# A shorter norm for the differential heads, and a part of the output projection moved ahead of the transposes

## The chip, the cores and the metric

The kernel runs on one core of one Trainium2 chip. Its time is the device time of that core in microseconds, as the median of three runs. One further execution was recorded by the hardware profiler; its rows give the times of single instructions, counted from the start of the recorded span.

## What is computed

One layer of an encoder over 528 rows (16 learned tokens, then 512 of the input) and 1,024 channels: two kinds of attention side by side, each with eight heads, then gates, an output projection and a feed-forward block. The change lies in the second kind, the differential attention: two softmax maps per head, one taken from the other, and a norm over the 128 channels of each head's result.

```python
def diff_attn_block(q, k, v, lam, slopes, qpos, kpos, qcid, kcid):
    s = einsum('bhcqd,bhckd->bhcqk', q, k) * (DF_HEAD_DIM ** -0.5)
    s = where(mask, s + bias, -inf)
    p = softmax(s, axis=-1)
    w = p[:, :, 0] - lam * p[:, :, 1]
    return einsum('bhqk,bhkd->bhqd', w, v)
...
o_df = rmsnorm(o_df, subln_g[l]) * (1.0 - lam_init)      # over the 128 channels of a head
y_sb = o_sb @ w_br_sb[l]
y_df = o_df @ w_br_df[l]
gates = sigmoid(xn @ w_gate[l] + b_gate[l])
merged = gates[:, :, 0] * y_sb + gates[:, :, 1] * y_df
h = h + merged @ w_out[l]
```

## The kernel before

**Matrix products.** Every product is made of high and low parts: `mm3` issues three matmuls (L296 high by high, L297 low by high, L298 high by low). Weights come from DRAM by SP's queue into one of three buffers `wst`; ACT casts the high part `wh` (L78, 128x1024), and DVE subtracts it from the weights to get the low part `wl` (L81). Both go to four buffers each.

**The order.** After a start whose order is written out, the instructions are handed to a scheduler, which orders each engine's by priority (mostly the order of the code) and by the times that it reckons. The code interleaves two streams. A head (`df_head`, a generator) makes its scores, maps and weighted sums, and stops at several places to yield a number. The loop over the heads then emits so many *units* of other work: the halves of the query, key and value projections of the head after it, and the parts of one projection unit `y`, which multiplies earlier heads' outputs by a block of `w_br_df` (`y_units`, four output blocks of six matmuls, 128x512; ACT copies each block out, L816, and POOL's queue sends it to DRAM, L818 or L820). `turn` turns the value projection. After each unit that a yield asks for stands a `tick`; every second one issues a background transfer on POOL's queue (L151, weights for the feed-forward part, mostly 512 KB), which waits for the last of ACT's casts when it was issued.

**A differential head.** `scores(0)` to `scores(2)` and `scores3` make the scores of four blocks of queries (L726 and L727 on PE), add the bias and take the maximum (L730 on DVE). `maps` takes the exponentials (L754 on ACT) and combines the two maps with DVE (L757 to L760, the last of them the combination `pr`, 528 columns wide for the last block). `turned` transposes the combined probabilities on PE (nine L581, then L582); the rest of its outputs are `a_h` (L591, ACT), `a_l` (L592, DVE) and the small corner `a_s` (`stk` L587, L598 on DVE, L601 on POOL). `av` makes the weighted sums (L604 to L614). Then the norm: `of` is the copy of the sums out of PSUM (L782), `sq` its square, split into `sqh` and `sql`, and two matmuls with the constant `ones_r` (L789, L790) add the squares over the 128 partitions. That second piece waits in the list `late` until the next head's first yield. Line L719 prepares the next head's bias on POOL, and L709 copies each of the two key components to the other 64 partitions by POOL's queue (264 KB each), once DVE's last L706 of that component is done; the next head's scores need them.

**The loop** (L1049 to L1066 of the file): in head 7, the last, there is no next head, so its units are its `y` unit and halves of the gates' products.

```python
        yield 3 if h < NH - 1 else 2
        turned()
        yield 2
        ps = av()
...
                units = units + more[0:1] + [turn] + more[1:]
...
            for n in head(h, d, o[0][:, h % 2], o[1][:, h % 2]):
                for _ in range(min(n, len(units))):
                    units.pop(0)()
                    tick(*RATE[br])
            for u in units:
                u()
```

The units of a head are four halves (query, key), two of the value projection's, and then, around `turn`, the two halves of `y`: each half is two output blocks. The yields ask for 1, 1, 1, 3 and 2 of these nine, and the last follows the head. The heads are counted from 0, so that head 4 is the fifth.

Of the kernel before, what the change touches and what calls it, by code (L numbers as in the profile page):

```python
# [9 lines left out]
F32 = mybir.dt.float32  # L10
F32R = mybir.dt.float32r
# [5 lines left out]
P = 128  # L17
D = 1024
SEQ = 512
# [22 lines left out]
def block_kernel(ctx: ExitStack, tc: tile.TileContext, x, meta, norm_mix_g, w_in, w_gate, b_gate,  # L42
# [34 lines left out]
    def split(hi, lo, src, lo_eng=None, hi_copy=None, after=None):  # L77
        cast["last"] = (hi_copy or nc.scalar.copy)(hi, src)  # L78
        if after:
            behind(cast["last"], after)  # L80
        cast["lo"] = (lo_eng or nc.vector).tensor_tensor(lo, src, hi.bitcast(F32), op=ALU.subtract)  # L81
# [634 lines left out]
    def df_head(h, d, o_h, o_l):  # L716
        q, k = d["q"], d["k"]
        bias = ap_.tile([P, L], F32, tag="bias", name="bias")
        nc.gpsimd.tensor_scalar(bias, dist, -(2.0 ** -(h + 1)), None, op0=ALU.mult)  # L719
        mx = small.tile([P, NQ, 2], F32, tag="mx", name="mx", bufs=2)  # L720
        ls = small.tile([P, NQ, 2], F32, tag="ls", name="ls", bufs=2)
        prs = [ap_.tile([P, 2, 144 + t * P], F32, tag=f"w{t}", name="pr") for t in range(NQ)]

        def score(o, t, c, k0, k1):
            qs = slice(t * P, (t + 1) * P)
            nc.tensor.matmul(o, lhsT=q[c][:, qs], rhs=k[c][:, 0, k0:k1], start=True, stop=False)  # L726
            nc.tensor.matmul(o, lhsT=q[c][:, qs], rhs=k[c][:, 1, k0:k1], start=False, stop=True)  # L727

        def biased(t, c, zz, po, bb):
            nc.vector.tensor_tensor_reduce(po, zz, bb, scale=1.0, scalar=-3.0e38, op0=ALU.add, op1=ALU.max,  # L730
                                           accum_out=mx[:, t, c:c + 1])

        def scores(t):
            n = 144 + t * P
            z = z_tile()
            for c in range(2):
                score(z[:, c, 0:max(n, 256)], t, c, 0, max(n, 256))
            for c in range(2):
                biased(t, c, z[:, c, 0:n], prs[t][:, c], bias[:, L - n:L])
            maps(t)  # L740

        def scores3(c):
            two = lambda v: v.rearrange("p (a b) -> p a b", a=2)
            z = z_tile()
            for hf in range(2):
                score(z[:, hf, 0:HL], 3, c, hf * HL, (hf + 1) * HL)
            biased(3, c, z[:, :, 0:HL], two(prs[3][:, c]), two(bias))

        def maps(t):
            pr = prs[t]  # L750
            nm = small.tile([P, 2], F32, tag="nm", name="nm")
            nc.vector.tensor_scalar(nm, mx[:, t], -1.0, None, op0=ALU.mult)
            for c in range(2):
                nc.scalar.activation(pr[:, c], pr[:, c], AF.Exp, bias=nm[:, c:c + 1], accum_out=ls[:, t, c:c + 1])  # L754
            with tc.high_priority(offset=EVAC):
                rc = small.tile([P, 2], F32, tag="rc", name="rc")
                nc.vector.reciprocal(rc, ls[:, t])  # L757
                nc.vector.tensor_tensor(rc, rc, cn, op=ALU.mult)
                nc.vector.tensor_scalar(pr[:, 0], pr[:, 0], rc[:, 0:1], None, op0=ALU.mult)
                nc.vector.scalar_tensor_tensor(pr[:, 0], pr[:, 1], rc[:, 1:2], pr[:, 0], op0=ALU.mult, op1=ALU.add)  # L760

        scores(0)
        scores(1)
        yield 1
        if late:
            late.pop(0)()
        scores(2)
        yield 1
        scores3(0)
        yield 1  # L770
        scores3(1)
        maps(3)
        turned, av = attn_out(lambda t, k0, k1: prs[t][:, 0, k0:k1], d, 64)
        yield 3 if h < NH - 1 else 2
        turned()
        yield 2
        ps = av()
        of = ap_.tile([P, SEQ], F32, tag="of", name="of")
        sq = ap_.tile([P, SEQ], F32, tag="sq", name="sq")
        sqh = ap_.tile([P, SEQ], F32R, tag="a_h", name="sqh")  # L780
        sql = ap_.tile([P, SEQ], F32R, tag="a_l", name="sql")
        nc.scalar.copy(of, ps)  # L782
        eng = nc.gpsimd if h < NH - 1 else nc.vector
        eng.tensor_tensor(sq, of, of, op=ALU.mult)
        split(sqh, sql, sq, lo_eng=eng)

        def norm():
            pv = tr_tile()
            nc.tensor.matmul(pv, lhsT=ones_r, rhs=sql, start=True, stop=False)  # L789
            nc.tensor.matmul(pv, lhsT=ones_r, rhs=sqh, start=False, stop=True)  # L790
            nc.scalar.activation(sq, pv, AF.Ln, bias=eps_c)
            cast["norm"] = nc.scalar.activation(sq, sq, AF.Exp, scale=-0.5)
            nc.vector.scalar_tensor_tensor(sq, pv, var_max, sq, op0=ALU.is_le, op1=ALU.mult)
            nc.vector.tensor_tensor(of, of, sq, op=ALU.mult)
            nc.scalar.activation(o_h, of, AF.Copy, scale=g_sub)
            nc.vector.scalar_tensor_tensor(o_l, of, g_sub, o_h.bitcast(F32), op0=ALU.mult, op1=ALU.subtract)

        late.append(norm)


    def y_units(name, i, o):

        def unit(fs):
            wh, wl = weights((name, i))
            for f in fs:
                ps = mm_tile()
                cs = slice(f % 4 * P, (f % 4 + 1) * P)
                mm3(ps, [(wh[:, k, cs], wl[:, k, cs], o[0][:, k], o[1][:, k]) for k in range(2)])
                if y_out:
                    ys = y_out[0][:, y_count[0] % KT]  # L810
                elif y_count[0] % 2:
                    ys = ap_.tile([P, SEQ], F32, tag="ys", bufs=2, name="ys")
                else:
                    ys = gate_tile(0)
                y_count[0] += 1
                nc.scalar.copy(ys, ps)  # L816
                if i < 2:
                    nc.gpsimd.dma_start(y_part[name][f], ys)  # L818
                else:
                    nc.gpsimd.dma_start(y_part[name][f], ys, accum_op=ALU.add)  # L820

        f0 = i % 2 * 4
        return [lambda: unit((f0, f0 + 1)), lambda: unit((f0 + 2, f0 + 3))]

    def gate(br, f, dst, func):
        def evac(ps):
# [200 lines left out]
    for br in range(2):  # L1027
        name, head = (("y_sb", sb_head), ("y_df", df_head))[br]
        if br:
            nc.gpsimd.memset(a_s, 0.0)  # L1030
            y_out.append(xtp.tile([P, KT, SEQ], F32, tag="y_sb", name="y_out"))
        for h in range(NH):
            if (br, h) == (0, 0):
                tB["t"] = opool.tile([P, 2, 2, 4, HL], F32R, tag="y_df", name="tB", bufs=1)
                sums = sum_units()
            if (br, h) == (0, 3):
                df_loads()
            if (br, h) == (0, 4):
                df_constants()
            if h % 2 == 0:  # L1040
                o = [opool.tile([P, 2, SEQ], F32R, tag=t, name=t) for t in ("o_h", "o_l")]
            if h + 1 < NH:
                nd, units, turn = (sb_units, df_units)[br](h + 1)
            elif br == 0:
                nd, units, turn = df_units(0)
            else:
                units, turn = [], None
            more = todo.pop(0) if todo else []
            if br == 0 and h < 2:  # L1049
                more = gate_out(h)  # L1050
            if turn is None:
                sg0 = [gate_tile(br) for br in range(2)]
                units = more + gate(0, 1, sg0[0], AF.Identity) + gate(1, 1, sg0[1], AF.Identity)
            else:
                units = units + more[0:1] + [turn] + more[1:]
            if (br, h) == (0, 0):
                for i, u in enumerate(sums):
                    units[i] = lambda a=units[i], b=u: (a(), b())
# [5 lines that stand above are left out]
                u()  # L1064
            d = nd
            if h % 2:  # L1066
                todo += [y_units(name, h - 1 + i, o) for i in range(2)]
    sg1 = [gate_tile(br) for br in range(2)]
    units = gate(0, 2, sg1[0], AF.Identity) + gate(1, 2, sg1[1], AF.Identity)
    units[0]()  # L1070
    late.pop(0)()
    for u in units[1:]:
        u()
    for units in todo:
        for u in units:
            u()
    for sg in sg0 + sg1:
        behind(nc.scalar.activation(sg, sg, AF.Sigmoid), "norm")
# [500 lines left out]
```

## Time and profile before

| | |
|---|---|
| runs | 932.18 us median of 3 (930.78 to 932.35) |
| the profiled execution | 930.21 us, of which the recorded span is 928.4 us |
| PE (matmul) | busy 916.8 us, 99% of the span, 6009 instructions |
| DVE | busy 741.2 us, 80% |
| ACT | busy 593.0 us, 64% |
| POOL | busy 171.6 us, 18% |
| granted TensorE clock | 0.999 |

The busy time of PE is modelled, since its matmuls are pipelined: two that follow each other without a gap are shown as overlapping, and the time that one costs is read from the distance between two starts. A row of the timeline gives the start, the length, the engine, the line, the operation with its output and inputs, and in brackets the idle time just before it and what ended it. The rows of the chain of waits have a start, a length, the engine, a tile, a line and a count. The rows by line and form give how often an instruction came, its shortest, median and longest time in nanoseconds, and from when to when.

### The profile page before, as it was taken

The page shows a single profiled execution, that of the slowest core. Times are in us where ns is not written, and L with a number is a line of the kernel's source. Part 1 is how long each engine was busy: PE and PEld are TensorE (multiplying, and loading weights), DVE is VectorE, ACT ScalarE, POOL GpSimd, SP SyncE. Part 2 cuts the span into 40 slices and gives each one's busy share as a digit, 9 for nine tenths or more (in the row PEclk, how much of TensorE's full clock was granted, in tenths as well). Part 3 has the DMA queues.
Part 4 walks back from the last instruction along what each step waited for, and adds up shares of the span by engine and source line. Part 5 has one row for each costly group of instructions (what it writes and reads, how often), then busy time and mean ns, then how long its engine had stood idle before and what let it go on. Part 6 is the DMA issues. An engine that isn't in the chain of part 4 may idle for free.

```text
span 928.4 us, 16121 instructions
## 1 busy us (share of the span) xinstructions
PE 916.8 (99%) x6009; PEld 834.1 (90%) x6010; DVE 741.2 (80%) x1453; ACT 593.0 (64%) x1136; POOL 171.6 (18%) x207
## 2 busy tenths in 40 slices
PE   8999999999999999999999999999999999999997
PEld 5999999998999899998988888899999999988886
DVE  7988877776687777977773787899888888799975
ACT  7665676676666766767665554776565655576554
POOL 4000121222333344344512000001100000000013
PEclk9999999999999999999999999999999999999999
DMA  8525698779776878799987774437744343276542
GB/s 253 143 74 159 147 211 202 168 168 257 185 203 157 218 180 195 172 206 179 207 207 173 214 271 155 123 87 182 172 122 128 91 133 96 91 272 195 192 148 91
DMA packets 155824, 158.42 MB, mean 171 GB/s; under 512 B 6465, under 2 KB 117218, under 8 KB 155746
## 3 DMA queue, kind: packets, MB, share of 16 engines
q1 hardware_dynamic: 132690, 101.61, 35.9%
q0 software_dynamic: 22896, 55.72, 28.9%
q8 instruction: 47, 0.77, 0.3%
q14 instruction: 31, 0.25, 0.1%
q10 hardware_dynamic: 160, 0.07, 0.0%
HBM read 133.64 MB, written 50.86 MB: 199 GB/s over the span
## 4 chain that ended last, share of the span: by engine, by line
PE 92%; DVE 4%; ACT 2%; issue 1%; DMA 0%; ACTq 0%; DVEq 0%
PE mm L296 22%; PE mm L297 22%; PE mm L298 22%; PE z L296 7%; PE z L297 7%; PE z L298 7%; PE z L581 2%; PE z L727 1%; PE z L726 1%; DVE wl L81 1%; PE tr L537 1%; DVE hres L1236 0%; ACT wh L78 0%; PE mm L889 0%; DMA wst<-in_w_ffn_up_dram 0%
## 5 line engine op out<-in xcount | busy, mean ns | idle before, releaser
L297 PE MATMUL mm<-xT_l,wh 128*128 128x264 f32 (+2 forms) x656 | 213.4, 325 | 0.5
L296 PE MATMUL mm<-xT_h,wh 128*128 128x264 f32 (+2 forms) x656 | 213.4, 325 | 0.5 <-ACT xT_h L932 0.5
L298 PE MATMUL mm<-xT_h,wl 128*128 128x264 f32 (+2 forms) x656 | 212.6, 324 | 0.0
L81 DVE TENSOR_TENSOR wl<-wst,wh 128x1024 fp32r<-128x1024 f32 (+1 forms) x147 | 163.2, 1115 | 27.7 <-ACT wh L78 27.3
L78 ACT CAST wh<-wst 128x1024 fp32r<-128x1024 f32 (+1 forms) x147 | 141.5, 966 | 58.8 <-PE mm L297 37.3
L297 PEld LDWEIGHTS mm<-xT_l,wh 128*128 128x128 f32 x656 | 123.4, 188 | 10.2 <-DVE xT_l L933 1.3
L298 PEld LDWEIGHTS mm<-xT_h,wl 128*128 128x128 f32 x656 | 123.5, 188 | 10.0
L296 PEld LDWEIGHTS mm<-xT_h,wh 128*128 128x128 f32 x656 | 123.4, 188 | 10.0 <-ACT xT_h L932 0.9
L296 PE MATMUL mm<-hT_h,wh 128*128 128x256 f32 x304 | 83.8, 277 | 0.3 <-ACT hT_h L1193 0.3
L298 PE MATMUL mm<-hT_h,wl 128*128 128x256 f32 x304 | 84.0, 277 | 0.0
L297 PE MATMUL mm<-hT_l,wh 128*128 128x256 f32 x304 | 83.9, 277 | 0.0
L296 PEld LDWEIGHTS mm<-hT_h,wh 128*128 128x128 f32 x304 | 56.9, 188 | 0.7 <-ACT hT_h L1193 0.5
L297 PEld LDWEIGHTS mm<-hT_l,wh 128*128 128x128 f32 x304 | 57.0, 188 | 0.0
L298 PEld LDWEIGHTS mm<-hT_h,wl 128*128 128x128 f32 x304 | 57.0, 188 | 0.0
L730 DVE CUSTOM_DVE_ANT_0 pr<-z,bias 128x144 f32<-128x144 f32 (+3 forms) x64 | 30.9, 502 | 30.5 <-PE z L727 28.5
L296 PE MATMUL mm<-o_h,wh 128*128 128x512 f32 x128 | 51.1, 399 | 0.0
L297 PE MATMUL z<-wl,da 128*128 128x512 f32 (+1 forms) x132 | 50.3, 381 | 0.2 <-DVE wl L81 0.2
L296 PE MATMUL z<-wh,da 128*128 128x512 f32 (+1 forms) x132 | 50.2, 380 | 0.0
L298 PE MATMUL z<-wh,da 128*128 128x512 f32 (+1 forms) x132 | 50.2, 380 | 0.0
L297 PE MATMUL mm<-o_l,wh 128*128 128x512 f32 x128 | 50.1, 391 | 0.0
L298 PE MATMUL mm<-o_h,wl 128*128 128x512 f32 x128 | 50.0, 391 | 0.0
L1481 POOL TENSOR_TENSOR outs<-hres,gF 128x512 f32<-128x512 f32 x4 | 6.2, 1549 | 217.2 <-DVE hres L1467 210.3
(388 smaller groups left out, 2509.9 us busy)
## 6 DMA issues: line engine op xcount, KB each, us to landing
wst<-in_w_in_dram SPq DMA_DIRECT2D x40, 512.0 KB, 6.0
ds<-in_w_ffn_down_dram POOLq DMA_DIRECT2D x30, 512.0 KB, 6.4
wst<-in_w_ffn_gate_dram SPq DMA_DIRECT2D x22, 512.0 KB, 3.9
wsu<-in_w_ffn_up_dram SPq DMA_DIRECT2D x20, 512.0 KB, 4.0
wst<-in_w_gate_dram SPq DMA_DIRECT2D x16, 512.0 KB, 5.0
y_df<-y_out POOLq DMA_DIRECT2D x32, 256.0 KB, 7.5
slots<-ds SPq DMA_DIRECT2D x13, 512.0 KB, 3.3
os<-in_w_out_dram POOLq DMA_DIRECT2D x12, 512.0 KB, 4.7
```

Of the source, the lines that this page charges most:

```text
L78: cast["last"] = (hi_copy or nc.scalar.copy)(hi, src)
L81: cast["lo"] = (lo_eng or nc.vector).tensor_tensor(lo, src, hi.bitcast(F32), op=ALU.subtract)
L296: nc.tensor.matmul(ps, lhsT=ah, rhs=bh, start=(start and i == 0), stop=False, skip_group_check=skip)
L297: nc.tensor.matmul(ps, lhsT=ah, rhs=bl, start=False, stop=False, skip_group_check=skip)
L298: nc.tensor.matmul(ps, lhsT=al, rhs=bh, start=False, stop=(stop and i == n - 1), skip_group_check=skip)
L537: nc.tensor.transpose(pt[:, j * P:(j + 1) * P], vT[:, j * P:(j + 1) * P], ident)
L581: nc.tensor.transpose(pt[:, (t - j) * P:(t - j + 1) * P], blocks(t, j * P, (j + 1) * P), ident)
L726: nc.tensor.matmul(o, lhsT=q[c][:, qs], rhs=k[c][:, 0, k0:k1], start=True, stop=False)
L727: nc.tensor.matmul(o, lhsT=q[c][:, qs], rhs=k[c][:, 1, k0:k1], start=False, stop=True)
L730: nc.vector.tensor_tensor_reduce(po, zz, bb, scale=1.0, scalar=-3.0e38, op0=ALU.add, op1=ALU.max, accum_out=mx[:, t, c:c + 1])
L1481: nc.gpsimd.tensor_tensor(outs[t][:, D1], hres[:, t, D1], gF[:, D1], op=ALU.mult)
```

## The change

Three things are done.

1. **The norm of heads 0 to 6.** Both halves of the partitions are squared apart: ACT squares `of[0:64]` into `sq2`, DVE squares `of[64:128]` into `sq[0:64]`, and DVE adds the two. ACT casts the high part of the 64 rows into `sqh[0:64]`, and DVE writes the low part into `sqh[64:128]`. One tile then holds both parts, and one matmul with `ones_r` adds them up. POOL has no part in it any more. Head 7 keeps square, split and two matmuls over all partitions.
2. **The projection unit.** In the differential branch it comes in three parts, of one, two and one output blocks. Every head now yields 4 ahead of `turned` (3 before, and 2 in head 7), so that the first block is emitted ahead of the transposes, the next two with `turn` between transposes and weighted sums, and the last after these. The list `todo` holds the arguments of a unit instead of the unit.
3. **The gates.** The first half of the gate product (0, 2) goes into the units of head 7.

With the larger yield a head has nine `tick`s instead of eight, and so two heads have nine background transfers instead of eight.

```diff
         turned, av = attn_out(lambda t, k0, k1: prs[t][:, 0, k0:k1], d, 64)
-        yield 3 if h < NH - 1 else 2
+        yield 4
         turned()
         yield 2
         ps = av()
...
-        sql = ap_.tile([P, SEQ], F32R, tag="a_l", name="sql")
         nc.scalar.copy(of, ps)
-        eng = nc.gpsimd if h < NH - 1 else nc.vector
-        eng.tensor_tensor(sq, of, of, op=ALU.mult)
-        split(sqh, sql, sq, lo_eng=eng)
+        halved = h < NH - 1
+        if halved:
+            A, B = slice(0, 64), slice(64, P)
+            sq2 = ap_.tile([P, SEQ], F32, tag="a_l", name="sq2")
+            nc.scalar.activation(sq2[A], of[A], AF.Square)
+            nc.vector.tensor_tensor(sq[A], of[B], of[B], op=ALU.mult)
+            nc.vector.tensor_tensor(sq[A], sq[A], sq2[A], op=ALU.add)
+            cast["last"] = nc.scalar.copy(sqh[A], sq[A])
+            cast["lo"] = nc.vector.tensor_tensor(sqh[B], sq[A], sqh[A].bitcast(F32), op=ALU.subtract)
+        else:
+            sql = ap_.tile([P, SEQ], F32R, tag="a_l", name="sql")
+            nc.vector.tensor_tensor(sq, of, of, op=ALU.mult)
+            split(sqh, sql, sq)
 
         def norm():
             pv = tr_tile()
-            nc.tensor.matmul(pv, lhsT=ones_r, rhs=sql, start=True, stop=False)
-            nc.tensor.matmul(pv, lhsT=ones_r, rhs=sqh, start=False, stop=True)
+            if not halved:
+                nc.tensor.matmul(pv, lhsT=ones_r, rhs=sql, start=True, stop=False)
+            nc.tensor.matmul(pv, lhsT=ones_r, rhs=sqh, start=halved, stop=True)
...
-    def y_units(name, i, o):
+    def y_units(name, i, o, parts=((0, 1), (2, 3))):
...
-        return [lambda: unit((f0, f0 + 1)), lambda: unit((f0 + 2, f0 + 3))]
+        return [lambda fs=fs: unit([f0 + f for f in fs]) for fs in parts]
...
-            more = todo.pop(0) if todo else []
+            more = y_units(*todo.pop(0), *(((0,), (1, 2), (3,)),)[0:br]) if todo else []
...
-                units = more + gate(0, 1, sg0[0], AF.Identity) + gate(1, 1, sg0[1], AF.Identity)
+                sg1 = [gate_tile(br) for br in range(2)]
+                third = gate(0, 2, sg1[0], AF.Identity)
+                units = more + gate(0, 1, sg0[0], AF.Identity) + gate(1, 1, sg0[1], AF.Identity) + third[0:1]
             else:
-                units = units + more[0:1] + [turn] + more[1:]
+                units = units + more[0:1 + br] + [turn] + more[1 + br:]
...
-    units = gate(0, 2, sg1[0], AF.Identity) + gate(1, 2, sg1[1], AF.Identity)
+    units = third[1:] + gate(1, 2, sg1[1], AF.Identity)
```

Behind the changed lines the numbers shift: the first line of the norm is L782 before and L781 after, the norm's last matmul L790 and L800, the copy of an output block L816 and L826.

At three places the order of the engines is shown. The first is PE's order at the transposes of head 4, before and then after; `o_h` and `o_l` are the outputs of earlier heads, so their rows are the projection unit's.

```order
L298 MATMUL mm<-xT_h,wl 128x264
L581 MATMUL z<-ident,pr 128x128 x9
L582 MATMUL z<-ident,pr 128x128
L296 MATMUL mm<-o_h,wh 128x512
L297 MATMUL mm<-o_l,wh 128x512
L298 MATMUL mm<-o_h,wl 128x512
```

```order
L298 MATMUL mm<-xT_h,wl 128x264
L296 MATMUL mm<-o_h,wh 128x512
L297 MATMUL mm<-o_l,wh 128x512
L298 MATMUL mm<-o_h,wl 128x512
L296 MATMUL mm<-o_h,wh 128x512
L297 MATMUL mm<-o_l,wh 128x512
L298 MATMUL mm<-o_h,wl 128x512
L581 MATMUL z<-ident,pr 128x128 x9
```

Six matmuls of the projection now stand between the last value projection and the first transpose.

The second is DVE's order in the same place, from the last but one weight subtraction before the probabilities to the row after their combination L760, before and then after.

```order
L81 TENSOR_TENSOR wl<-wst,wh 128x1024
L706 SCALAR_TENSOR_TENSOR dqk<-mm,dqk 64x264
L757 RECIPROCAL rc<-ls 128x2
L587 TENSOR_TENSOR stk<-pr,stk 64x16
L758 TENSOR_TENSOR rc<-rc,cn 128x2
L598 STREAM_TRANSPOSE a_s<-stk 32x32
L759 TENSOR_SCALAR pr<-pr,rc 128x528
L706 SCALAR_TENSOR_TENSOR dqk<-mm,dqk 64x264
L760 SCALAR_TENSOR_TENSOR pr<-pr,rc 128x528
```

```order
L81 TENSOR_TENSOR wl<-wst,wh 128x1024
L587 TENSOR_TENSOR stk<-pr,stk 64x16 x2
L598 STREAM_TRANSPOSE a_s<-stk 32x32 x4
L757 RECIPROCAL rc<-ls 128x2
L598 STREAM_TRANSPOSE a_s<-stk 32x32 x2
L758 TENSOR_TENSOR rc<-rc,cn 128x2
L706 SCALAR_TENSOR_TENSOR dqk<-mm,dqk 64x264
L759 TENSOR_SCALAR pr<-pr,rc 128x528
L81 TENSOR_TENSOR wl<-wst,wh 128x1024
L760 SCALAR_TENSOR_TENSOR pr<-pr,rc 128x528
L706 SCALAR_TENSOR_TENSOR dqk<-mm,dqk 64x264
```

More of the corner's rows and one more weight subtraction stand ahead of L760, and the last L706, which the second key copy follows, stands behind it.

The third is POOL's order from head 4's bias to its corner, before and then after; the rows L709 are the two key copies.

```order
L719 TENSOR_SCALAR bias<-dist 128x528
L151 DMA ds_2_97<-in_w_ffn_down_dram 256x1x512
L709 DMA dqk<-dqk 64x1056 x2
L601 CAST a_sr<-a_s 128x256
```

```order
L719 TENSOR_SCALAR bias<-dist 128x528
L709 DMA dqk<-dqk 64x1056
L151 DMA ds_8_100<-in_w_ffn_down_dram 256x1x512
L709 DMA dqk<-dqk 64x1056
L601 CAST a_sr<-a_s 128x256
```

A background transfer now stands between the two copies. Around the copy `of` of head 6, ACT's order changes in the same manner: before, the cast of the squares `sqh` came directly behind the copy, and now the square `sq2` and a cast of weights stand between them.

More of the change, by code (lines that the diff above doesn't have):

```diff
@@ L1066, in block_kernel @@
             if h % 2:
-                todo += [y_units(name, h - 1 + i, o) for i in range(2)]
-    sg1 = [gate_tile(br) for br in range(2)]
-    units = gate(0, 2, sg1[0], AF.Identity) + gate(1, 2, sg1[1], AF.Identity)
+                todo += [(name, h - 1 + i, o) for i in range(2)]
+    units = third[1:] + gate(1, 2, sg1[1], AF.Identity)
     units[0]()
@@ L1073, in block_kernel @@
         u()
-    for units in todo:
-        for u in units:
+    for args in todo:
+        for u in y_units(*args):
             u()
```

## The prediction

> **What bounds the kernel.** I read the page first, then PE's waits and the windows of the differential heads, then the timelines of one head (head 4, the fifth of eight) on PE, DVE, ACT and POOL.
>
> ```profile
> span 928.4 us, 16121 instructions
> PE 916.8 (99%) x6009; PEld 834.1 (90%) x6010; DVE 741.2 (80%) x1453; ACT 593.0 (64%) x1136; POOL 171.6 (18%) x207
> ...
> PE 92%; DVE 4%; ACT 2%; issue 1%; DMA 0%; ACTq 0%; DVEq 0%
> ...
> 361.50:391.00 29.50, 29.49 (x194) 27.00 (x193) 22.94 (x67) 20.65 (x49) 12.08 (x15) 1.00 0.84 187
> 450.00:476.00 26.00, 26.00 (x136) 22.21 (x136) 18.47 (x60) 19.11 (x47) 11.95 (x14) 1.00 1.08 223
> ```
>
> PE is busy 99% of the span and ends the chain for 92% of it. The window rows give busy time of PE, PEld, DVE, ACT, POOL, then granted clock (1.00), DMA share and GB/s: in head 4 PE never idles, DVE works 22.9 of 29.5 us, and in head 6 the DMA share is 1.08. So only two things move the end: fewer PE instructions, and holes in PE's stream. In a dense stream a matmul is worth the distance between starts, not its shown length:
>
> ```profile
> 463.10 0.39 PE L789 MATMUL tr<-sql,ones_r 128*128 128x512 f32 x1
> 463.33 0.39 PE L790 MATMUL tr<-sqh,ones_r 128*128 128x512 f32 x1
> 463.56 0.34 PE L726 MATMUL z<-dqk 128*128 128x400 f32 x1
> ```
>
> 0.39 us long each, but 0.23 apart. The holes are at the transposes L581. The chain has these runs, of which the one at 272.83 (head 0) did not wait:
>
> ```profile
> 272.83 0.98 PE z L581 x9
> 302.20 1.18 PE z L581 x9
> 331.87 1.10 PE z L581 x9
> 361.37 0.33 PE z L581 x3
> 361.70 0.87 PE z L581 x6
> 391.07 1.10 PE z L581 x9
> 420.57 1.17 PE z L581 x9
> 450.23 1.10 PE z L581 x9
> ...
> 476.21 0.49 PE L581 MATMUL z<-ident,pr 128*128 128x128 f32 x3
> 477.12 0.88 PE L581 MATMUL z<-ident,pr 128*128 128x128 f32 x6 [0.42 <-DVE pr L760]
> 477.83 0.27 PE L582 MATMUL z<-ident,pr 128*128 128x128 f32 x1
> ```
>
> Heads 1 to 6 lose 0.20, 0.12, 0.22, 0.12, 0.19 and 0.12, together 0.97 us, against 0.98. Head 7 takes 477.83 - 476.21 = 1.62 for the nine, 0.64 too long. What they wait for is DVE's last combination of the probabilities, L760.
>
> **The change, part by part.**
>
> *One norm matmul less in heads 0 to 6.* 7 x 0.23 = -1.6 us, straight off PE's stream. The Trainium skill ("TensorE: Matmul & The Clock Gate", section Back-to-back issue gap) gives a sustained 131 ns for 512 columns and 216 ns isolated, so the term would be -0.9 or -1.5 by it; the trace's 0.23 decides.
>
> *Three half-height DVE operations and an ACT square for two POOL operations.* Half height saves no time:
>
> ```profile
> L699 DVE SCALAR_TENSOR_TENSOR dqk<-mm,dqk 64x512 fp32r<-64x512 f32 x2 | 1.4, 688 | 0.1
> L784 DVE TENSOR_TENSOR sq<-of x1: 693/693/693, 483.6 to 483.6; 128x512 f32<-128x512 f32 x1
> L78 ACT CAST sqh<-sq x8: 620/620/622, 281.0 to 484.3; 128x512 fp32r<-128x512 f32 x8
> L1240 ACT ACTIVATE sq<-hres x8: 627/632/634, 579.8 to 599.9; 128x512 f32<-128x512 f32 x8
> 371.42 0.31 DVE L730 CUSTOM_DVE_ANT_0 pr<-z,bias 128x144 f32<-128x144 f32 x1 [4.06 <-PE z L727]
> 386.90 1.22 DVE L81 TENSOR_TENSOR wl<-wst,wh 128x1024 fp32r<-128x1024 f32 x1
> 390.47 0.77 DVE L760 SCALAR_TENSOR_TENSOR pr<-pr,rc 128x528 f32<-128x528 f32 x1
> 390.91 1.26 PE L581 MATMUL z<-ident,pr 128*128 128x128 f32 x9
> ```
>
> So 3 x 0.69 = 2.1 us more on DVE per head (25.0 of 29.5 us) and 0.63 on ACT; POOL's share is idle time won for nothing. Square and addition fall into DVE's 4.06 us of idleness before L730; the subtraction (0.69) does not, and delays the probabilities behind it.
>
> *The first quarter of the projection unit goes ahead of the transposes.* A quarter is six matmuls of 0.23, 1.36 us, on PE at no cost since it only changes place. It gives L760 1.36 us, less 0.23 for the missing norm matmul: the transposes of head 4 start at 390.91 + 1.36 - 0.23 = 392.04, and the fourth, which needs L760, at 392.37. L760 itself: ahead of the last L730 DVE now has the subtraction (0.69) and one L760 of 400 columns (0.62) more, and one wl (1.22) and two stk with four transposes (1.1) less, so that L730, at 385.08 before, starts about 384.0. Behind it stand in order 0.64 (L730), 0.43, 0.16, wl 1.22, stk and six transposes 1.6, 0.32, 0.43, 0.50, wl 1.22 and L760 0.77, 7.3 us, with some 0.03 between each 7.6. L760 ends near 391.6, 0.8 us ahead of need. I count on -0.9 of the 0.97; the ends are -0.97 (all hidden) and, if the walk is 2 us off, +1.2 x 6 = +7.
>
> *Head 7.* Behind its last scores stand now four gate halves (10.9 us) and not two (5.4), so that the 0.64 goes: -0.64. But fewer matmuls stand ahead of head 6's norm: a quarter (1.36), scores (0.98), a quarter (1.36), together 3.7 us after the end of the weighted sums, where two halves and the scores were 6.4. The operands' chain, from head 4's rows:
>
> ```profile
> 367.89 0.40 PE L296 MATMUL mm<-o_h,wh 128*128 128x512 f32 x1
> 368.09 0.59 ACT L782 COPY of<-z 128x512 f32<-128x512 f32 x1 [0.63 <-PE z L614]
> 370.64 0.28 PE L726 MATMUL z<-dk,dq 128*128 128x256 f32 x1
> 370.84 1.05 ACT L78 CAST wh<-wst 128x1024 fp32r<-128x1024 f32 x1
> ```
>
> The sums end at 367.89, and the copy 0.79 later. The square (0.63) ends at 1.45, the addition at 2.2. Now a weight cast stands ahead of sqh on ACT. Its buffer was freed by the unit behind the sums (370.64, cast at 370.84), so it starts at 1.36 + 0.2 and ends at 2.6; sqh ends at 3.2, the subtraction at 3.95. The norm would start at 4.0 and not 3.7: +0.4 with the restart (0 to +0.7). In heads 0 to 5 a whole query half (2.72) stands there, and the norm has 1.1 us to spare. Head 7's own norm keeps its chain and its cover.
>
> *The key copies on POOL.* The last L706 stands behind L760 and no longer before it:
>
> ```profile
> 387.80 1.11 POOL L151 DMA_DIRECT2D ds<-in_w_ffn_down_dram  x1
> 388.88 0.60 POOL L709 DMA_DIRECT2D dqk<-dqk  x1
> 390.74 0.54 POOL L709 DMA_DIRECT2D dqk<-dqk  x1 [1.26 <-DVE dqk L706]
> ...
> DMA to landing us min/median/max: 2.9/7.2/8.4
> 400.23 0.28 PE L726 MATMUL z<-dqk 128*128 128x256 f32 x1
> ```
>
> L706 ends at 391.6 + 0.43 instead of 390.43, so the second copy is issued near 392.3, 1.5 us later; with the median 7.2 it lands at 399.5. The scores that need it, 400.23 less the norm matmul and the hole, come at 399.9, the second component's at 400.1. So it is just hidden; at the maximum 8.4 it is 0.6 late. I take +0.2, with 0 and +6 as ends (below).
>
> *The rest at nothing.* Half a unit more per head also lets half a background transfer more go: 512 KB at POOL's 1.1 us, taken out of the time after the heads, where PE is full. POOL has 17 of 29.5 us free in head 4 to cover it. The gate half that moves into head 7 takes its weights 2.7 us earlier; PE waits for no weight tile in the heads now.
>
> **Sum:** -1.6 - 0.9 - 0.64 + 0.4 + 0.2 = -2.5 us. The profiled execution took 930.21 (span 928.4 and 1.8 around it), 2.0 below the median 932.18 of the three runs, which reach from 930.78 to 932.35; so I set the difference against the median: 929.7.
>
> **Rivals.**
>
> *A: the key copies come late (slower).* A background transfer now stands between the two copies on POOL's queue. If the second waits for POOL's 1.1 us too, and takes the 8.4, it lands at 401.8, 1.7 us after need. Four heads (3 to 6) have the high DMA share: +6.8 in place of +0.2, 936.3. It decides for slower once the copies cost over 1 us in each of those four heads. For it: the share of 1.08, latencies close to the slack. Against it: POOL sends the transfer while it waits for L706 anyway (it idled 1.26 us there). The Trainium skill ("DMA: Bandwidth & Descriptors", section Two DMAs through the same engine are not ordered) says descriptors of one queue start in order, which speaks for this rival; no row here shows the order inside a queue.
>
> *B: DVE gets no earlier.* The 2.1 us come back as the same holes in heads 1 to 6: -1.6 - 0.64 + 0.4 + 0.2 = -1.6, 930.6. For it: DVE at 85% and 0.8 us of margin at the end of a walk of twenty. Against it: 1.36 us more cover.
>
> *C: everything hidden,* head 6's norm and the copies too: -1.6 - 0.97 - 0.64 = -3.2, 929.0.
>
> **Chances.** 0.2% is 1.9 us, about what can be told from no change. Forecast 0.45, C 0.17, B 0.25, A 0.13. B and half a microsecond of noise in either median leave the first two below 930.3 four times in five, B one time in four: faster 0.57. A is slower in two of three cases, 0.09; the rest, 0.34, is within 0.2%. The range goes from C less the noise, 928.3, to B with the mild A on top, 932.3, where the copies cost 1.7 us more; the forecast's own is 928.9 to 930.6.
>
> **What would show it.** In the trace after: L790's successor L800 alone, seven L799 gone; each run of nine L581 at 0.98 (if 1.1 and more, B); the first L726 of a head directly behind the last projection matmul (if PE waits there for a DMA of dk or dqk, A); head 6's L800 waiting 0.3 for DVE L790. DVE's busy time in a head should be 25.0 us. The prediction is wrong if DVE's L760 comes over 1 us later than walked, or if a copy lands after 400.

## The result, and the profile after

The changed kernel takes 929.82 us (median of 22 runs) against 931.7 us (22 runs of the kernel before beside them): a ratio of 0.9982, with a 95% interval from 0.9973 to 0.999, so 1.7 us less, between 0.9 and 2.5. Forecast were 2.5 us less and 929.7. The profiled execution took 929.71 us, span 927.9.

The same views as before, first the page and the windows of head 4 and of the end of head 6 to head 7 (PE, PEld, DVE, ACT, POOL, clock, DMA share, GB/s):

```profile
span 927.9 us, 16073 instructions
PE 915.9 (99%) x6002; PEld 833.9 (90%) x6003; DVE 752.5 (81%) x1474; ACT 595.4 (64%) x1143; POOL 156.6 (17%) x193
...
362.40:391.59 29.19, 28.80 (x190) 26.38 (x188) 24.63 (x69) 20.35 (x50) 11.33 (x14) 1.00 0.96 206
451.20:476.00 24.80, 24.80 (x125) 20.85 (x124) 20.69 (x63) 18.59 (x45) 9.15 (x11) 1.00 1.09 246
```

PE has seven matmuls less, a head takes 29.2 us and not 29.5, and DVE works 24.6 of them (22.9 before). The chain shows what became of the holes at the transposes:

```profile
303.40 0.99 PE z L581 x9
332.81 0.98 PE z L581 x9
361.90 8.45 DMA dk<-dk
391.87 0.98 PE z L581 x9
421.04 0.98 PE z L581 x9
450.24 0.98 PE z L581 x9
477.61 0.98 PE z L581 x9
```

All are gone, head 7's too. Head 3's nine are not on the chain, and take 0.99 (361.81 to 362.80). In their place stands a key copy, 8.45 us from issue to landing, and PE waits for it at the next head's scores:

```profile
369.61 0.28 PE L726 MATMUL z<-dk,dq 128*128 128x256 f32 x1
369.73 0.28 PE L727 MATMUL z<-dk,dq 128*128 128x256 f32 x1
370.40 0.39 PE L726 MATMUL z<-dk,dq 128*128 128x256 f32 x1 [0.39 <-DMA dk<-dk]
...
460.00 0.39 PE L298 MATMUL mm<-o_h,wl 128*128 128x512 f32 x1
460.37 0.50 PE L800 MATMUL tr<-sqh,ones_r 128*128 128x512 f32 x1
460.71 0.34 PE L726 MATMUL z<-dqk 128*128 128x400 f32 x1
```

The first three rows are the scores of the head after head 3: 0.67 us between the second and the third where 0.11 is the step. The next three are head 6's norm, at a distance of 0.37 and 0.34 where 0.23 is the step.

To set kernels apart by less than the runs do, I take one stretch of PE: from its first score (the first L726 of head 0) to its first transpose of the feed-forward part (tile hn). All that the change touches lies in it. The rows of before and after (count, durations, first and last start):

```profile
L726 PE MATMUL z<-dk,dq x40: 276/284/345, 252.9 to 441.1; 128*128 128x264 f32 x16, 128*128 128x256 f32 x8, 128*128 128x272 f32 x8, 128*128 128x400 f32 x8
L1188 PE MATMUL z<-ident,hn x32: 272/273/328, 592.6 to 611.4; 128*128 128x128 f32 x32
```

```profile
L726 PE MATMUL z<-dk,dq x40: 276/285/390, 252.9 to 439.8; 128*128 128x264 f32 x16, 128*128 128x256 f32 x8, 128*128 128x272 f32 x8, 128*128 128x400 f32 x8
L1199 PE MATMUL z<-ident,hn x32: 270/273/329, 590.4 to 609.5; 128*128 128x128 f32 x32
```

339.7 us before, 337.5 after: 2.1 us less (339.68 and 337.53 by the unrounded starts). That the span is only 0.5 shorter has its cause behind the stretch, in this one execution. Windows of before, then of after, in the feed-forward part:

```profile
610.00:620.00 10.00, 10.00 (x90) 10.00 (x90) 8.93 (x18) 6.39 (x9) 0.00 (x0) 1.00 0.06 15
```

```profile
610.00:620.00 10.00, 10.00 (x87) 10.00 (x86) 9.89 (x17) 7.47 (x10) 0.00 (x0) 1.00 0.01 2
```

PE waits in neither, but did 87 matmuls in 10 us and not 90, and so on from about 607 to 643 us, which makes 1.3 us of the 1.6 that are missing. Such stretches come and go: in a second profiled execution of the changed kernel (below) there is none.

### The profile page after: what moved, and what is told of

Its sections match the earlier page's. It is cut to its first block, busy times and chain, and to the rows that moved or that the text cites. A ratio compares the mean times of both kernels' runs of the same rounds, so it can differ in the third digit from the quotient of the medians.

```text
span 927.9 us, 16073 instructions
## 1 busy us (share of the span) xinstructions
PE 915.9 (99%) x6002; PEld 833.9 (90%) x6003; DVE 752.5 (81%) x1474; ACT 595.4 (64%) x1143; POOL 156.6 (17%) x193
## 4 chain that ended last, share of the span: by engine, by line
PE 93%; DVE 3%; ACT 2%; DMA 1%; issue 1%; ACTq 0%; DVEq 0%
PE mm L297 22%; PE mm L296 22%; PE mm L298 22%; PE z L297 7%; PE z L296 7%; PE z L298 7%; PE z L581 2%; PE z L726 1%; PE z L727 1%; DMA dk<-dk 1%; PE tr L537 1%; DVE wl L81 1%; DVE hres L1247 0%; ACT wh L78 0%; DMA wst<-in_w_ffn_up_dram 0%
## 5 line engine op out<-in xcount | busy, mean ns | idle before, releaser
L81 DVE TENSOR_TENSOR wl<-wst,wh 128x1024 fp32r<-128x1024 f32 (+1 forms) x147 | 163.8, 1119 | 29.6 <-ACT wh L78 29.5
L754 ACT ACTIVATE pr<-pr,nm 128x144 f32<-128x144 f32 (+3 forms) x64 | 36.3, 568 | 19.8 <-DVE nm L752 19.8
```

## The experiments

In the tables "stretch" is that part of PE's stream against before's 339.68 us, from one profiled execution; "ratio" is that of the runs.

### One part at a time

Norm alone: before with `halved` and its branch, nothing else.

```diff
-        eng.tensor_tensor(sq, of, of, op=ALU.mult)
-        split(sqh, sql, sq, lo_eng=eng)
+        halved = h < NH - 1
+        if halved: ...   # as in the change
```

> The kernel before with the half-height norm of heads 0 to 6 and nothing else: units, yields and gates stay as before. Theory A (the parts need each other: what the norm adds to DVE pushes the combined probabilities, and only the projection block moved ahead of the transposes covers that): 1.6 us of matmuls go, but each head's L760 comes up to 0.7 us later (the subtraction stands ahead of it) and PE arrives 0.23 earlier, so the runs of nine L581 in heads 1 to 6, 0.97 us of holes before, have 3 to 6 us; the time is the same as before or up to 4 us longer (931 to 936). Theory B (the parts are independent, DVE has room): the holes stay near 1 us and the kernel gains 1.6 us (about 930.1).

Order alone: the changed kernel with the old norm, square and low part on POOL.

```diff
-        halved = h < NH - 1
-        if halved: ...
+        eng = nc.gpsimd if h < NH - 1 else nc.vector
+        eng.tensor_tensor(sq, of, of, op=ALU.mult)
+        split(sqh, sql, sq, lo_eng=eng)
```

> The changed kernel with the full norm of before (square and low part on POOL, two matmuls): only the projection unit's split, the larger yields and the gate half are left. Theory A: all transposes run without a hole (0.98 us for nine, head 7 too), 1.6 us gained; the norm's operands in head 6, by the rows of before 3.9 us after the weighted sums, miss the 3.7 us that stand ahead of them by 0.3, or 1.3 if a weight cast goes ahead of them: net -0.3 to -1.3, about 930.8. DVE's last L706 comes early enough that no background transfer lies between the two key copies, so no wait at the scores. Theory B (key copies are late because two heads have nine background transfers for eight, wherever they stand): the same wait at the scores as in the changed kernel, 0.5 to 0.8 us in all.

Order with the full norm on DVE: the changed kernel with

```diff
-        halved = h < NH - 1
+        halved = False
```

> The changed kernel with the full norm (two matmuls) in all heads, its square and low part on DVE: against the changed kernel one full-height operation less on DVE and one matmul more on PE per head. Theory A (the order alone was slower since POOL's norm is slow): no holes at the transposes and the weighted sums, 7 x 0.23 = 1.6 us more than the changed kernel, 0.5 less than before. Theory B (the order alone was slower because the scheduler, by its own reckoning, puts a query's low parts, o_l and a weight subtraction ahead of the last block's maximum on DVE, and so a_l comes late): the same order stands here, holes of 0.2 to 0.7 us at the start of each head's weighted sums, 1 to 2 us longer than before.

| kernel | stretch | ratio (95%) |
|---|---|---|
| norm alone | +0.8 | 1.0023 (1.0010 to 1.0036) |
| order alone, norm on POOL | +1.6 | 1.0023 (1.0013 to 1.0033) |
| order, full norm on DVE | -1.1 | 1.0004 (0.9988 to 1.0021) |
| both (the change) | -2.1 | 0.9982 (0.9973 to 0.9990) |

Each part alone makes the kernel slower by its runs, and both together make it faster. The chain and a timeline of the norm alone:

```profile
302.58 0.87 PE z L581 x6
...
477.85 0.87 PE z L581 x6
...
391.06 0.49 PE L581 MATMUL z<-ident,pr 128*128 128x128 f32 x3
391.83 0.87 PE L581 MATMUL z<-ident,pr 128*128 128x128 f32 x6 [0.28 <-DVE pr L760]
392.54 0.27 PE L582 MATMUL z<-ident,pr 128*128 128x128 f32 x1
```

The nine take 392.54 - 391.06 = 1.48 us in head 4 (0.98 without a hole): 0.50 where before lost 0.12. So theory A of the norm alone holds in its mechanism, in every head from 1 on. Its size is at the low end: heads 1 to 6 have 3.3 us of holes where theory A gave 3 to 6. With head 7, 1.6 us of matmuls go and 2.4 of holes are added. The square and the addition fall into DVE's idle time, and the subtraction moved L760 by 0.4, within the 0.7 given: from the last score's start to the end of L760 head 3 takes 9.24 us before (352.41 to 361.65) and 9.59 here.

The order alone lost most, some 1.7 us, where neither theory had it, at the weighted sums. The rest is theory A's wait at head 6's norm (0.4) and theory B's for a key copy (0.7, at head 5's scores alone). The last score of head 3 and the DVE rows that follow, order alone and then the change:

```profile
353.63 0.28 PE L727 MATMUL z<-dqk 128*128 128x264 f32 x1
...
354.29 0.76 DVE L796 SCALAR_TENSOR_TENSOR o_l<-of,g_sub,o_h 128x512 fp32r<-128x512 f32 x1
...
355.15 0.69 DVE L699 SCALAR_TENSOR_TENSOR dq<-mm,dq 64x512 fp32r<-64x512 f32 x1
...
356.75 0.69 DVE L730 CUSTOM_DVE_ANT_0 pr<-z,bias 128x528 f32<-128x528 f32 x1
...
363.14 0.77 DVE L760 SCALAR_TENSOR_TENSOR pr<-pr,rc 128x528 f32<-128x528 f32 x1
...
367.27 1.55 DVE L592 TENSOR_TENSOR a_l<-z,a_h 128x512 fp32r<-128x512 f32 x3 [0.79 <-ACT a_h L591]
```

```profile
351.63 0.28 PE L727 MATMUL z<-dqk 128*128 128x264 f32 x1
...
353.54 0.69 DVE L730 CUSTOM_DVE_ANT_0 pr<-z,bias 128x528 f32<-128x528 f32 x1
...
360.12 0.75 DVE L760 SCALAR_TENSOR_TENSOR pr<-pr,rc 128x528 f32<-128x528 f32 x1
```

With the norm on POOL the scheduler lets `o_l` and both queries' low parts run between this score and the last maximum on DVE: L730 starts 3.12 us after the score. In the change `o_l` and one of the low parts start before the score, and it is 1.91. L760 ends 10.28 us after the score (9.24 in the change), though DVE has less to do. The block moved ahead lets the transposes start later, so they show no hole, but `a_l` comes late behind them: in the chain of this kernel L592 takes the place of L581 in four heads, and PE waits 0.2 to 0.7 us at the weighted sums. With the norm on DVE at full height L760 ends 9.87 us after the score (352.96 to 362.83), and this suffices: no hole at transposes or sums, and 0.5 us of wait for a key copy. So theory A of the third kernel is borne out (POOL's norm is what hurts; by the stretch, with 1.1 us less than before, it is even 0.6 better than that theory's sum, while its runs are the same as before's), though its order on DVE is like that of the order alone, as theory B had it. The late maximum by itself is not the cause. It is as late in the kernel before and with the norm on DVE:

```profile
355.49 0.69 DVE L730 CUSTOM_DVE_ANT_0 pr<-z,bias 128x528 f32<-128x528 f32 x1
...
356.17 0.71 DVE L730 CUSTOM_DVE_ANT_0 pr<-z,bias 128x528 f32<-128x528 f32 x1
```

These are 3.08 and 3.21 us after their scores (352.41 and 352.96), yet L760 ends 9.24 and 9.87 after them. That taking the norm off POOL removes the holes is shown; by which step POOL's norm makes L760 and `a_l` late is not, since no run changed DVE's order by itself.

### The key copies

Key copies ahead: the low parts of the last key half are kept, and each background transfer waits for them. A counter `held` also keeps back those that fall due just ahead of the second copy, so that none is sent between the two copies or shortly ahead of them. In the trace a head's transfers then go out in a bunch behind the second copy (head 4's five from 390.79 to 396.68).

```diff
+        if "keys" in cast:
+            tc.add_manual_dep(ds, cast["keys"].ins.name, paced)
...
+                cast["keys"] = nc.vector.scalar_tensor_tensor(k[c][a, 1, s], ps[a], scale, ...
```

> The changed kernel, with the background transfer that stands between the two key copies of a head moved behind the second; number of transfers and all else unchanged. Theory A (the second copy shares the DMA engines with the 512 KB issued just ahead of it): the second copy lands some 3 to 6 us after its issue and not 8, PE waits nowhere for dk or dqk, and the 0.8 us of holes at the scores of heads 2 and 4 go: 929.0. Theory B (it is late because DVE's last L706 is late and the DMA engines are loaded in any case): its latency stays near 8 us, the holes stay, 929.8.

Two transfers between the copies: two are issued behind the first copy in heads 1 to 6, and the ticks of the head leave out two.

```diff
+                    if c == 0 and h:
+                        cast["keys"] = lo
+                        for _ in range(min(2, len(background))):
+                            background.pop(0)()
+                            held[0] -= 1
```

> The changed kernel with two background transfers between the two key copies of heads 1 to 6 and not one; their number over all stays, others in the head are left out for it. Theory A: the second copy has twice the transfer ahead of it and lands 11 to 14 us after its issue, 3 to 5 us after the scores need it: holes of 3 to 5 us in each of the heads 2 to 7, the kernel 15 to 25 us slower than the changed one. Theory B (the copy's latency depends on the load, not on what was issued just ahead of it): latency 8 to 9 us, holes under 1 us per head, at most 5 us slower.

The time of all copies from issue to landing in heads 1 to 6 (least, median, most), for the even heads' tile: first the change, then two between, and third a later kernel with the copies ahead. The last two rows are the kernel before, and the slowest copy of the order alone, from its chain:

```profile
DMA to landing us min/median/max: 3.0/5.5/8.5
```

```profile
DMA to landing us min/median/max: 3.0/5.8/10.3
```

```profile
DMA to landing us min/median/max: 3.0/4.6/5.3
```

```profile
DMA to landing us min/median/max: 5.8/6.8/8.4
...
393.06 9.97 DMA dqk<-dqk
```

Over both tiles the second copies take 3.9 to 4.8 us with the copies ahead, 6.9 to 8.5 in the change, with one transfer between, and 8.5 to 10.5 with two. But a place between the copies is not what makes a copy slow. The kernel before and the order alone have no transfer between, only one that is sent 1.1 to 2.4 us ahead of both copies, and their second copies take 5.8 to 8.4 and 5.6 to 10.0 us. What the kernel with the copies ahead shows is that a copy lands within theory A's 3 to 6 us when no transfer was sent shortly before it. PE's waits follow. With the copies ahead it has no wait for keys. With two between:

```profile
PE z L737 <- DMA dk<-dk: 3.3, 3, 2.3
PE z L737 <- DMA dqk<-dqk: 2.8, 2, 2.1
...
402.00:407.60 5.60, 3.53 (x23) 3.02 (x22) 1.85 (x6) 3.35 (x6) 1.00 (x2) 1.00 1.07 223
407.60:410.60 3.00, 3.00 (x9) 2.33 (x8) 2.94 (x12) 0.91 (x4) 0.00 (x0) 0.51 1.13 214
```

The stretch grows by 7.1 us against before (ratio 1.0084, 1.0071 to 1.0097), by 9.3 against the change. The result lies between the theories: a second transfer ahead does delay the copy, by 0.4 to 2.5 us from head to head (1.4 in the mean) and not by theory A's 3 to 6. Whether the copy waits its turn in the queue or shares the DMA engines, these runs do not tell. A part of the loss is the clock: after a pause of 2.1 us the granted clock was 0.51 for three us (last row), eight matmuls at 0.43 us each.

The copies ahead did what theory A says, up to the end of the heads: the last norm matmul starts 232.9 us after the first score and not 233.8 (485.60 - 252.71 and 486.67 - 252.89). But the stretch is only 0.9 us shorter than before, 1.2 longer than the change, and the runs show no gain (ratio 0.9996, 0.9985 to 1.0007). A new wait took the place, told by ACT and PE:

```profile
483.86 0.62 ACT L78 CAST sqh<-sq 128x512 fp32r<-128x512 f32 x1 [0.76 <-DVE sq L801]
487.92 1.05 ACT L78 CAST wh<-wst 128x1024 fp32r<-128x1024 f32 x1 [3.44 <-DMA wst<-in_w_gate_dram]
...
489.46 0.68 ACT L809 ACTIVATE sq<-tr,eps_c 128x512 f32<-128x512 f32 x1
...
471.43 16.13 DMA wst<-in_w_gate_dram
...
PE mm L304 <- ACT o_h L813: 1.3, 1, 1.3
```

The transfers held back ran in head 7 beside the gate's weights, which took 16.13 us to land (10.8 in the change). ACT stood at their cast, the last norm's logarithm (L809) stood behind the cast, and the projection unit that needs `o_h` waited.

### Without transfers in head 7

Two kernels leave head 7's transfers, all but one, to the feed-forward part, and hold the sigmoids behind the last `o_h`. The second has two more edits:

```diff
-        if late:
-            late.pop(0)()
         scores(2)
+        if late:
+            late.pop(0)()
...
+            nc.tensor.matmul(pv, lhsT=ones_r, rhs=sqh, start=True, stop=halved)
             if not halved:
-                nc.tensor.matmul(pv, lhsT=ones_r, rhs=sql, start=True, stop=False)
-            nc.tensor.matmul(pv, lhsT=ones_r, rhs=sqh, start=halved, stop=True)
+                nc.tensor.matmul(pv, lhsT=ones_r, rhs=sql, start=False, stop=True)
```

> The kernel in which the key copies go ahead of the background transfer, without the three background transfers that stood in head 7 (all but one are left to the feed-forward part, as many as there were before the change), and with the gates' sigmoids held behind the last head's o_h. Theory A (the gate's weights came 16 us late because these transfers, 17 to 22 us each, shared the DMA engines; ACT stood 3.4 us at their cast, and the last norm's logarithm behind it): the weights land within 11 us, PE does not wait at the last projection unit, and from the first scores of head 0 to the feed-forward part the kernel is 3.0 us shorter than before (2.1 of the change and 0.9 for the key copies): 928.9. Theory B (the gate's weights are late because SP's queue sends them where it does): the 2.0 us at the last projection unit stay: 930.9.

> As the kernel with key copies ahead and head 7 without the transfers, and in addition each head's norm is emitted behind the third block's scores and not ahead of them, and the two matmuls of head 7's norm change places, so that the high part's runs while DVE still makes the low part. Theory A: head 6's norm, 0.25 us late in the changed kernel, gets 0.9 us more cover and does not wait; head 7's low part is waited for as before but the high part's 0.23 lies in that wait; 0.25 + 0.24 us less than without the two edits, 3.5 us shorter than before: 928.4. Theory B (what is moved on PE comes back as later operands on DVE, since the norm's last steps move behind the third block's bias): holes at the transposes or the weighted sums of 0.1 to 0.5 us per head, no gain or up to 2 us longer.

The stretch came as theory A has it: 3.0 and 3.7 us shorter than before. But both kernels are slower, by ratios of 1.0092 (1.0073 to 1.0110) and 1.0085 (1.0062 to 1.0109). My edit sent the five transfers that were left at one time. Of the first kernel, POOL, the chain and PE:

```profile
631.18 4.48 POOL L151 DMA_DIRECT2D ds<-ds  x5 [5.98 <-ACT q L1368]
...
634.89 13.99 DMA wsu<-in_w_ffn_up_dram
...
651.12 0.58 PE L304 MATMUL z<-hT_h,wh 128*128 128x256 f32 x1 [8.85 <-DVE qy L1384]
```

A load of weights stands on the chain with 13.99 us, and PE waited 8.85. With one at a time (`held[0] = 0` behind the loop), and the changed kernel beside them:

> As the kernel with the key copies ahead and head 7 without background transfers, except that the feed-forward part issues the transfers left over one at a time, as before the change, and not five at once. Theory A (the 8.8 us that PE waited in the feed-forward part came from the five transfers sent at once, ahead of a load of weights): that wait goes, nothing else changes: 3.0 us shorter than before up to the feed-forward part and at the end, about 928.7. Theory B (the feed-forward part has no room for transfers that the heads leave over): a wait of some us stays there, 930 or more.

> The same with the norm behind the third block's scores and the two matmuls of head 7's norm exchanged. Theory A: 3.6 us shorter than before up to the feed-forward part, as its heads were with the five transfers at once, and no wait after it: about 928.1 and the shortest of all. Theory B: a wait in the feed-forward part stays, 930 or more.

> The changed kernel itself once more, beside the two others on the same chip: 1.9 us shorter than before (1.0 to 2.8), and a second trace of it: up to the feed-forward part 2.1 us shorter than before again, with one wait of 0.5 to 0.7 us for a key copy and 0.25 at head 6's norm; whether the 37 to 50 us in which PE ran 4% slower after 596 us in its first trace come again at the same place.

| kernel | stretch | median | ratio (95%) |
|---|---|---|---|
| key copies ahead, head 7 free | -3.0 | 929.18 | 0.9954 (0.9939 to 0.9968) |
| the same, two edits at the norm | -3.7 | 929.70 | 0.9960 (0.9945 to 0.9976) |
| the change again | -2.3 | 930.94 | 0.9977 (0.9962 to 0.9993) |
| before, beside them | 0 | 932.93 | 1 |

The 8.85 us are gone, and both kernels have the stretch that theory A gave them. They beat before; against the change they are 0.8 and 1.4 us shorter by the stretch, while the intervals of the runs overlap. In the second's heads no wait of PE is left that the view of its waits shows.

The 0.7 us that it has over the first don't show in the medians. In its profiled execution the first score came 3.3 us later (256.2), with waits in the first 160 us that the others don't have.

The change again has the same waits: 0.46 and 0.31 us at the scores of heads 2 and 4, none at the transposes. Its span is 927.2, and PE keeps 90 matmuls in 10 us where the first trace had 87 (that row is above).

### Two blocks ahead

The projection unit in two halves, one ahead of the transposes, none behind the sums: the list of parts left out, and `more[0:1] + [turn] + more[1:]`.

> The changed kernel with the projection unit in two halves, the first half (two blocks) ahead of the transposes and the second between them and the weighted sums; none is left behind the sums. Theory A (one block is all the cover that the probabilities need, and the block behind the sums covers the norm): the transposes gain nothing more, and the norm of heads 0 to 5 has 3.7 us ahead of it for operands that take 4.0, head 6's 2.3: 0.3 us per head and 1.7 in head 6, the kernel 2 to 4 us longer than the changed one. Theory B (the scheduler fills in other work and the norm is not late): the same time as the changed kernel within 0.5 us.

The stretch is 5.6 us longer than before and 7.7 longer than the change, the ratio 1.0061 (1.0041 to 1.0080). Theory A, with 2 to 4 us, did not have the greater part: some 6 us of the 7.7 are in head 7, whose units are used up before the sums, so that its norm has nothing beside it:

```profile
PE tr L799 <- DVE sql L81: 3.6, 1, 3.6
...
492.00:496.50 4.50, 4.46 (x11) 3.49 (x12) 1.44 (x2) 3.14 (x4) 0.00 (x0) 0.50 0.43 120
```

After the 3.6 us of wait the granted clock is 0.50 for 4.5 us. In the heads before, theory A's 0.3 us per head are there: from transposes to transposes they take 29.5 us, where the change has 29.2, both without the waits for keys.

## Why the prediction was right

The direction, the place of the gain and most terms came as forecast; how near the time itself came, 929.8 to 929.7, owes something to luck. The 2.5 us were counted from the median of three runs, 932.18, and 22 runs of before have 931.7. The errors of the terms cancel in part. And the times alone do not tell the forecast from rival B: its 1.6 us lie in the middle of the runs' interval (0.9 to 2.5), the forecast's 2.5 at the edge. The trace tells them apart, by 0.98 for the nine transposes in every head. By the terms:

- **One norm matmul less, -1.6.** Right: the profile has seven matmuls less at 0.23. That this is "straight off PE's stream" holds only with the cover: alone, the norm gave 2.4 back.
- **The three half-height operations.** They take 0.69, 0.68 and 0.68 us, as at full height, and DVE works 24.6 us in head 4 (25.0 forecast). The time won on POOL was worth more than the "nothing" that the prediction gave it: with the blocks moved, the norm on POOL has a stretch 2.7 us longer than the same norm on DVE (+1.6 and -1.1).
- **The transposes, -0.9.** All 0.97 went. L760 of head 4 ended at 390.65 and not "near 391.6", 1.39 us ahead of the fourth transpose (392.04), not 0.8. The walk set the last L730 at 384.0, and it started at 383.31; the rows behind it took 7.3 us and not 7.6.
- **Head 7, -0.64.** Right: 0.98 for its nine.
- **Head 6's norm, +0.4.** Right in its cause, the weight cast ahead of `sqh` on ACT; 0.25 measured, and gone when the norm stands behind the third block's scores.
- **The key copies, +0.2.** Right in kind, too small: 0.9 in the first trace (0.66 at 369.73 to 370.62, of which the rows above show the first part, and 0.22 at the scores of head 2), 0.8 in the second. This is the mis-sized term. The walk set one median latency of 7.2 against one slack; the second copies had 6.9 to 8.5 and the slack is about zero, so that some heads wait and others do not. Head 4's copy, the one walked, landed at 399.38, ahead of need and of the sign at 400; heads 1 and 3 had the late ones. That a transfer stands between the copies was no new burden by itself, since before had one ahead of both; but in heads 1 to 5 the second copies are issued 0.5 to 1.7 us later than before, and over heads 1 to 6 they take 1.0 us longer in the mean. The Trainium skill ("DMA: Bandwidth & Descriptors", section Two DMAs through the same engine are not ordered), by which descriptors of a queue start in order, was counted for rival A. The runs show that transfers sent ahead make the second copy later (up to 4.8 us with none shortly ahead, 8.5 and 10.5 with one and two between), but not whether by order or by sharing.
- **The rest at nothing.** The background transfers in head 7 cost PE no wait here. In the kernel with the copies ahead, which sent eight between 449 and 479 us where the change sent four, the gate's weights were late.

The sum by what was measured is -1.6 - 0.97 - 0.64 + 0.25 + 0.9 = -2.1, and the stretch has -2.1 and -2.3. The runs' -1.7 (0.9 to 2.5) holds it. Rivals A and B did not come about; C was out of reach by the keys and head 6, and the last kernel, which mends both, has its -3.2 and a little more (-3.7).

## What to carry to other kernels

A saved matmul on a full engine is worth its time only if its neighbours' operands come no later: price the work that the saving moves to another engine, and move some independent matmuls ahead of the place that waits, in one and the same change. Two parts that each lose can win together, so a part that is slower alone is no proof against it. On a shared DMA queue a small copy that someone waits for goes ahead of the bulk, and bulk that is put off must not come back all at once.

## What the runs showed of the hardware

- PE ran 4% slower for some 40 us in six of the thirteen profiled executions (86 or 87 matmuls in 10 us and not 90) while the granted clock column shows 1.00. It came in the feed-forward part, at different places or not at all. Its cause is open, and so is how often it comes in the runs without a profile; 1.3 us in one execution is most of what this change is worth.
- The granted clock fell to half for about 3 to 4.5 us after pauses of PE of 2.1 and 3.6 us. A pause of 2.3 us in the kernel with two transfers (at 372 us) was followed by 1.00:

```profile
375.00:378.00 3.00, 3.00 (x16) 2.65 (x17) 2.29 (x11) 0.49 (x3) 0.20 (x1) 1.00 1.11 211
```

  The Trainium skill ("TensorE: Matmul & The Clock Gate", section Part 1: The HAM clock gate) has the clock halve after an idle window of about 3.4 us that runs freely. The free-running window fits the one pause with and the other without; that 2.1 us were enough is less than the page says, and the measurement decides.
- A 264 KB copy takes 3.0 us when no transfer was sent shortly before it, and up to 10.5 behind two of 512 KB. A 512 KB load of the gate's weights took 7.0 to 10.8 us in the change's head 7, and 16.1 to 21.4 where eight transfers from DRAM to DRAM had been bunched.
